# A hybrid decoder block: the last group's gathered rows go to another buffer, a group sooner, and its weights are made ahead of the merges

## The chip, the cores and the metric

The kernel runs on one core of a Trainium2 chip. It is written by hand for the core's engines: PE (TensorE, matrix products into PSUM banks), ACT (ScalarE), DVE (VectorE), POOL (GpSimd, here mostly the issuer of indirect gathers) and SP (SyncE, which issues direct loads and stores; ACT issues some as well). Each engine works through its own instructions in the order written; semaphores order them across engines. The metric is the time of one execution on the device in microseconds, the median over several runs; lower is better.

## The reference

One layer on 256 tokens of width 2048, in float32. First token mixing (RG-LRU and Mamba-2 heads between two projections), then a PEER mixer, then a final norm. The change touches only the end of the PEER mixer and the final norm:

```python
def peer(h, w_q, sub_keys, u_tab, v_tab):
    ...                                  # product keys: 16 experts of 128*128 for each of 8 heads
        u = jnp.take(u_tab, e, axis=0)
        act = jax.nn.gelu(jnp.einsum("td,thkd->thk", xt, u).astype(jnp.float32))
        v = jnp.take(v_tab, e, axis=0)
        return jnp.einsum("thk,thkd->td", (g * act).astype(v.dtype), v)
...
    return x + gate2 * peer(h2, peer_w_q, peer_sub_keys, peer_u, peer_v)
...
    return rms_norm(x, final_norm_g)
```

So each token needs a weighted sum of 8 x 16 = 128 rows of `v_tab` (2048 numbers each), whose weights are the gate times the gelu of a score, the score being the product of the token with a row of `u_tab`.

## The kernel before

**Two ways to one sum.** The kernel orders the experts with the second key's index as the slow one. Experts with slow index below `J1 = 80` are done *sparsely*: all scores of all tokens with these experts are computed as dense products and stored in DRAM (`ad`); then, token by token, the 128 scores and the 128 rows of `v_tab` that the token needs are gathered by indirect DMA. The other 48 slow indices (`JD = 48`) are done *densely*: scores with all of them (`u_slot`), a matrix of weights `Wt[0]`, `Wt[1]` (24 slow indices each, 128 x 24 x 256), and then dense products with the value table (`v_slot`), in two column halves `h` of 48 slots each.

**The sparse part.** Tokens go in 64 groups of four, one for each 32-row strip of the output tile; groups 0 to 31 make the first 128 tokens (`tb` = 0), groups 32 to 63 the second. For a group `q`:

- `w_gather` (line 1370) issues one gather of 128 scores, a column of the tile `wA`; four make a group. `v_gather` (line 1362) issues one gather of 128 rows, 8 KB each, into one of eight buffers `vs[n % 8]`, so two groups lie in memory at a time. Numbers past the table are left out by the bounds check (they are the dense ones). Both go to POOL's queue.
- `w_make` (line 1379) makes the four weight columns: a gelu on ACT (line 1383), then a product with the gates on DVE into `Wz` (line 1387). `Wz` has three places (`NW = 3`), and the columns around the four are zero, so that a window of 32 columns moves each token's sum to its own row of the strip.
- `v_quad` (line 1389) does 16 products on PE (line 1397): for each of four column blocks `c` (one PSUM bank each), the four tokens `g`. Token `g` uses PE's columns and the bank's rows 32 g to 32 g + 31, so neighbouring products go to different strips of PE. Each product is float32 and makes two matmul records. The sums stay in four banks over 32 groups.

`sparse()` (line 1409) does a group: one score gather, `v_quad`, then row and score gathers in turn, for the rows of group q + 2 and the scores ahead. Its weights for the next group are put on the list `late` and made at the next `tick`. A row gather waits until PE has read the buffer that it fills.

**The dense part.** `v_slot` (line 1470) first splits a later slot's weights into a high and a low part (`split_to`, ACT line 442 and DVE line 443), then does 12 matmuls on PE (line 1483) into four banks, two for each half of the tokens, then issues the splitting of a later value tile (`issue_split`, ACT line 144, DVE line 153), whose DVE step also issues the next load.

**The order around the change.** `tick` (line 1421) is called twice in each dense score slot and once after each value slot, 192 times in all; it decides by the count whether a `sparse()` comes, in the second part about once in three value slots. Group 61 comes just before the last value slot; groups 62 and 63 come behind it, at the end of the kernel. `mid()` runs steps that were deferred. `merge(tb, c, ps)` (line 1503) multiplies a bank by the gate (1505), adds it to the rows of the residual `R["t"]` (1507), and when both sums of a column block are in, takes the squares on ACT (1510). It is done for four banks behind the last value slot of each half, and for four banks behind groups 31 and 63. `final(tb)` (line 1512) multiplies two column blocks by the norm's weights (1516), makes the root (1518 to 1520), scales and stores: two blocks by ACT (1525), two by DVE (1523), and three stores on SP (1526, 1527). At the end the order before is: weights of 63, deferred steps, `final(0)`, group 63 with its merges, `final(1)`.

Of the kernel before, what the change touches and what calls it, by code (L numbers as in the profile page):

```python
# [15 lines left out]
OP = mybir.AluOpType  # L16
# [42 lines left out]
def hybrid_kernel(ctx, tc, xT, cols, w_ada, w_in, lru_w, w_o1, w_o2, w_q, keys, u_t, v_t, fng, out):  # L59
# [1299 lines left out]
    def tok(q, g):  # L1359
        return (q // 32) * 128 + 32 * g + q % 32  # L1360

    def v_gather(n):
        q, g = divmod(n, 4)
        if q >= 64:
            return
        x, t = vs[n % 8], tok(q, g)
        pool.indirect_dma_start(x, None, vf, bass.IndirectOffsetOnAxis(ap=eV[:, t:t + 1], axis=0),  # L1367
                                bounds_check=E1 - 1, oob_is_err=False)
# [9 lines left out]

    def w_make(q):
        if q >= 64:  # L1380
            return
        a = wA[:, 4 * q:4 * q + 4]
        act.activation(a, a, AF.Gelu_apprx_tanh)
        tb, m = divmod(q, 32)
        g = gT[:, tb * 128:(tb + 1) * 128].rearrange("p (g m) -> p g m", g=4)[:, :, m]
        o = Wz[:, 32:].rearrange("p (n c) -> p n c", c=32)[:, 4 * (q % NW):4 * (q % NW) + 4, 0]
        dve.tensor_tensor(o, a, g, op=OP.mult)  # L1387

    def v_quad(q):
        tb, m = divmod(q, 32)  # L1390
        if m == 0:
            for c in range(4):
                sb[c] = bank(c)
        for c in range(4):
            for g in range(4):
                x = 32 + 32 * (4 * (q % NW) + g) - m
                pe.matmul(sb[c][32 * g:32 * g + 32, :], Wz[:, x:x + 32], vs[4 * (q % 2) + g][:, c * 512:(c + 1) * 512],  # L1397
                          start=(m == 0), stop=(m == 31), skip_group_check=True)
        if m == 31:
            for c in range(4):  # L1400
                merge(tb, c, sb[c])
# [7 lines left out]
    def sparse():  # L1409
        q = sq["n"]  # L1410
        if q < 64:
# [3 lines left out]
            for g in range(4):  # L1415
                if g:
                    w_gather()
                v_gather(4 * q + 8 + g)
# [51 lines left out]
    def v_slot(h, jj):  # L1470
# [8 lines left out]
        for tb in range(2):  # L1479
            s = slice(tb * 128, (tb + 1) * 128)  # L1480
            for i, k in ((0, 0), (1, 0), (0, 1)):
                for c in range(2):
                    pe.matmul(ob[tb * 2 + c], w[:, i, s], v[:, k, c * 512:(c + 1) * 512],  # L1483
                              start=(jj == 0 and (i, k) == (0, 0)), stop=(jj == JD - 1 and k == 1))
        if jj == JD - 1:
# [17 lines left out]
    def merge(tb, c, ps):  # L1503
# [5 lines left out]
        if R[tb, c] == 2:  # L1509
            act.activation(ps, a, AF.Square, accum_out=rf[:, tb, c:c + 1])  # L1510

    def final(tb):
        a, fn, rows = R["t"][:, tb], R["t"][:, 2], out[tb * 128:(tb + 1) * 128, :]
        for c in range(2):
# [52 lines left out]
    while sq["n"] < 63:  # L1567
        tick()
        sparse()
    tick()  # L1570
    mid()
    mid()
    final(0)
    sparse()
# [70 lines left out]
```

## Time and profile before

| what | value |
|---|---|
| median of 3 runs | 2152.05 us (2142.25 to 2161.91) |
| the profiled execution, its own time | 2157.51 us |
| its span | 2155.8 us |
| PE busy | 2085.5 us, 97% of the span |
| DVE, ACT, POOL busy | 1397.8, 964.9, 887.8 us |
| DMA | 620.54 MB, mean 288 GB/s |
| line 1397 (sparse sums on PE) | 2048 matmul records, two for each product |
| line 1483 (dense sums on PE) | 1152 matmul records, 276.9 us busy |
| score gathers, row gathers on POOL | 256 and 256 |

How to read it: times are microseconds from the start of the span. "PE" is the matmul, "PEld" the loading of its weights, which runs beside it. Behind a row, in brackets, stands how long the engine had been idle before it and what ended that idle time; "issue" means nothing that the profile shows. The ends of matmuls are modelled, and some matmul records can be missing. A row that names POOL with DMA_INDIRECT is the issuing of a gather, not its transfer. Names such as `tk` and `vq` are the eight row buffers (0 to 3 and 4 to 7), `X` in a score gather is the tile `wA`, `H` at the end is the tile of the residual rows.

### The profile page before, as it was taken

Reading aid. Unit: us, or ns where it says so; the run is one execution under the profiler, and the core shown is the slowest. Engines: PE = TensorE matmul, PEld = TensorE weight load, DVE = VectorE, ACT = ScalarE, POOL = GpSimd, SP = SyncE. Lnnn points to the kernel's source line nnn. Section 1 sums busy time; section 2 is a strip of 40 time slices with the busy share of each in tenths; the row PEclk is TensorE's granted clock in tenths of the full one; section 3 lists DMA queues with packets and bytes.
Section 4 is the critical chain, followed back from the end, with each engine's and each line's share of the span. In section 5 each row is a group of like instructions: output and inputs, shape, how many; then the busy total and the mean of one; then the engine's idle time right before and its main releaser. Section 6 shows DMA issues by size and latency. Waiting matters only on the chain.

```text
span 2155.8 us, 34802 instructions
## 1 busy us (share of the span) xinstructions
PE 2085.5 (97%) x13060; PEld 1633.2 (76%) x13060; DVE 1397.8 (65%) x2009; ACT 964.9 (45%) x1472; POOL 887.8 (41%) x728
## 2 busy tenths in 40 slices
PE   7999999999999999999999999999999999999996
PEld 4789989988999898888788778666666656555653
DVE  3378887977888869779889986433334353343434
ACT  3356656666644454444445444333333333333332
POOL 0013133412112110002325641777777757777774
PEclk9999999999999999999999999999999999999998
DMA  9967666767789955677777778899999999999996
GB/s 388 406 224 247 211 218 224 257 223 247 265 306 344 323 181 176 202 242 254 253 259 234 237 266 282 302 360 339 334 348 348 345 329 344 359 371 345 347 342 232
DMA packets 250615, 620.54 MB, mean 288 GB/s; under 512 B 38024, under 2 KB 122168, under 8 KB 228152
## 3 DMA queue, kind: packets, MB, share of 16 engines
q1 hardware_dynamic: 188992, 387.76, 52.0%
q0 software_dynamic: 45056, 175.52, 22.3%
q10 hardware_dynamic: 16400, 55.06, 7.7%
q8 instruction: 102, 1.67, 0.3%
q14 instruction: 65, 0.53, 0.1%
HBM read 696.60 MB, written 14.72 MB: 330 GB/s over the span
## 4 chain that ended last, share of the span: by engine, by line
PE 70%; DMA 9%; DVE 9%; issue 5%; ACT 3%; POOL 2%; another core or an unknown queue 1%; SPq 0%; POOLq 0%; DVEq 0%; ACTq 0%
PE b L449 14%; PE b L1397 9%; PE b L1483 7%; PE b L451 7%; PE b L1323 4%; PE b L1325 4%; PE b L1324 4%; DVE hl L153 4%; PE b L918 3%; DMA raw<-in_w_in 2%; PE b L796 2%; PE b L797 2%; PE b L798 2%; PE b L919 1%; DMA adw<-in_w_ada 1%
## 5 line engine op out<-in xcount | busy, mean ns | idle before, releaser
L144 ACT ACTIVATE hl<-raw 128x1024 fp32r<-128x1024 f32 x594 | 628.0, 1059 | 1058.4 <-PE b L451 198.2
L153 DVE TENSOR_TENSOR hl<-raw,hl 128x1024 fp32r<-128x1024 f32 x594 | 764.7, 1297 | 133.9 <-ACT hl L144 119.5
L449 PE MATMUL b<-H,hl 128*128 128x512 f32 x1376 | 495.1, 403 | 0.1
L451 PE MATMUL b<-H,hl 128*128 128x256 f32 x1376 | 386.8, 281 | 3.9 <-DVE hl L153 3.6
L1376 POOL DMA_INDIRECT X<-ad,X x256 | 297.2, 1161 | 87.7 <-issue 74.4
L449 PEld LDWEIGHTS b<-H,hl 128*128 128x128 f32 x1376 | 259.6, 189 | 87.1 <-issue 19.2
L1483 PE MATMUL b<-hl,X 128*128 128x512 f32 x1152 | 276.9, 397 | 12.3 <-ACT X L442 9.7
L1483 PEld LDWEIGHTS b<-hl,X 128*128 128x128 f32 x1152 | 213.7, 189 | 88.3 <-issue 27.3
L451 PEld LDWEIGHTS b<-H,hl 128*128 128x128 f32 x1376 | 261.0, 190 | 6.5 <-DVE hl L153 5.0
L1323 PE MATMUL b<-hl,H 128*128 128x512 f32 x640 | 253.3, 396 | 0.0
L1325 PE MATMUL b<-hl,H 128*128 128x512 f32 x640 | 250.3, 391 | 2.5 <-DVE hl L153 2.5
L1324 PE MATMUL b<-hl,H 128*128 128x512 f32 x640 | 250.2, 391 | 0.0
L1367 POOL DMA_INDIRECT vq<-in_v_t,X x128 | 150.0, 1172 | 112.8 <-DVE vq L1537 39.0
L1367 POOL DMA_INDIRECT tk<-in_v_t,X x128 | 144.8, 1132 | 70.9 <-issue 32.3
L798 PE MATMUL b<-H,hl 128*128 128x256 f32 x560 | 160.2, 286 | 4.4 <-DVE hl L153 4.4
L796 PE MATMUL b<-H,hl 128*128 128x256 f32 x560 | 163.3, 292 | 0.0
L797 PE MATMUL b<-H,hl 128*128 128x256 f32 x560 | 159.9, 286 | 0.0
L1387 DVE TENSOR_TENSOR Wz<-X 128x4 f32<-128x4 f32 x64 | 10.8, 169 | 224.7 <-DMA X<-ad,X 98.6
L1325 PEld LDWEIGHTS b<-hl,H 128*128 128x128 f32 x640 | 120.6, 188 | 29.2 <-DVE hl L153 4.0
L389 DVE SCALAR_TENSOR_TENSOR adacc<-adr,cact,adacc 128x1024 f32<-128x1024 f32 x90 | 127.6, 1418 | 19.3 <-DMA adr<-in_w_ada 19.0
L1323 PEld LDWEIGHTS b<-hl,H 128*128 128x128 f32 x640 | 120.6, 188 | 23.9
L1324 PEld LDWEIGHTS b<-hl,H 128*128 128x128 f32 x640 | 120.6, 188 | 23.9
(324 smaller groups left out, 3163.2 us busy)
## 6 DMA issues: line engine op xcount, KB each, us to landing
raw<-in_u_t SPq DMA_DIRECT2D x208, 512.0 KB
raw<-in_w_in SPq DMA_DIRECT2D x146, 512.0 KB
adr<-in_w_ada SPq DMA_DIRECT2D x96, 512.0 KB
adw<-in_w_ada SPq DMA_DIRECT2D x64, 512.0 KB
raw<-in_w_o SPq DMA_DIRECT2D x64, 512.0 KB
raw<-in_u_t ACTq DMA_DIRECT2D x48, 512.0 KB
raw<-in_v_t SPq DMA_DIRECT2D x48, 512.0 KB
raw<-in_v_t ACTq DMA_DIRECT2D x48, 512.0 KB
```

Of the source, the lines that this page charges most:

```text
L144: act.activation(t[:, 0], r, AF.Copy)
L153: dve.tensor_sub(t[:, 1], r, t[:, 0].bitcast(FT))
L449: pe.matmul(ps, w[:, 0, c], x[:, k].rearrange("p a b -> p (a b)"), start=(k == first), stop=False, skip_group_check=True)
L451: pe.matmul(ps[:, :256], w[:, 1, c], x[:, k, 0], start=False, stop=(k == 15), skip_group_check=True)
L796: pe.matmul(ps, wh, hT[:, k, 0, :], start=(k == 0), stop=False)
L798: pe.matmul(ps, wl, hT[:, k, 0, :], start=False, stop=(k == 15))
L1323: pe.matmul(o, hh, w[:, 0, :, kk], start=(k == 0), stop=False)
L1324: pe.matmul(o, hl_, w[:, 0, :, kk], start=False, stop=False)
L1325: pe.matmul(o, hh, w[:, 1, :, kk], start=False, stop=(k == 15))
L1367: pool.indirect_dma_start(x, None, vf, bass.IndirectOffsetOnAxis(ap=eV[:, t:t + 1], axis=0), bounds_check=E1 - 1, oob_is_err=False)
L1376: pool.indirect_dma_start(wA[:, n:n + 1], None, adf, bass.IndirectOffsetOnAxis(ap=eW[:, t:t + 1], axis=0), bounds_check=T * E1 - 1, oob_is ...
L1483: pe.matmul(ob[tb * 2 + c], w[:, i, s], v[:, k, c * 512:(c + 1) * 512], start=(jj == 0 and (i, k) == (0, 0)), stop=(jj == JD - 1 and k == 1))
```

## The change

Six edits, all in the sparse part and the end:

- Rows 253, 254 and 255 (tokens 1 to 3 of group 63) go to the place of `Wt[0]`, which holds 3 x 2048 numbers for each partition and is read for the last time about value slot 23 of the second half. Their gathers are issued after group 60, behind its own four; row 252 keeps its buffer and is gathered after group 61.
- At groups 20, 26, 32 and 38 one more score gather is issued, so that from then on scores run four further ahead; the last is issued at group 60.
- In the last value slot, ahead of its merges, the waiting weights (group 62) and those of group 63 are made; `made` keeps them from being made twice.
- `v_quad` takes its 16 products in another order for two groups: group 61 by token (0, 1, 2, 3) with the four column blocks inside, group 63 by token (1, 2, 3, 0).
- The final norm's product for the first two column blocks of the first 128 tokens is done on DVE two deferred steps after their merge, in the middle of the value slots, and no longer in `final(0)`.
- At the end groups 62 and 63 are issued one behind the other, then the deferred steps and `final(0)`, then group 63's four merges and `final(1)`.

```diff
+    def row(n):
+        if n < 253:
+            return vs[n % 8]
+        return Wt[0].rearrange("p a b -> p (a b)")[:, (n - 253) * D:(n - 252) * D]
+
     def v_gather(n):
...
-        x, t = vs[n % 8], tok(q, g)
+        x, t = row(n), tok(q, g)
...
+    made = set()
+
     def w_make(q):
-        if q >= 64:
+        if q >= 64 or q in made:
             return
+        made.add(q)
...
-        for c in range(4):
-            for g in range(4):
-                x = 32 + 32 * (4 * (q % NW) + g) - m
-                pe.matmul(sb[c][32 * g:32 * g + 32, :], Wz[:, x:x + 32], vs[4 * (q % 2) + g][:, c * 512:(c + 1) * 512],
-                          start=(m == 0), stop=(m == 31), skip_group_check=True)
-        if m == 31:
+        order = [(c, g) for c in range(4) for g in range(4)]
+        if q == 61:
+            order = [(c, g) for g in range(4) for c in range(4)]
+        if q == 63:
+            order = [(c, g) for g in (1, 2, 3, 0) for c in range(4)]
+        for c, g in order:
+            x = 32 + 32 * (4 * (q % NW) + g) - m
+            pe.matmul(sb[c][32 * g:32 * g + 32, :], Wz[:, x:x + 32], row(4 * q + g)[:, c * 512:(c + 1) * 512],
+                      start=(m == 0), stop=(m == 31), skip_group_check=True)
+        if q == 31:
             for c in range(4):
                 merge(tb, c, sb[c])
...
-                v_gather(4 * q + 8 + g)
+                if q != 61 or not g:
+                    v_gather(4 * q + 8 + g)
+            if q == 60:
+                for g in range(1, 4):
+                    v_gather(252 + g)
+            if q in (20, 26, 32, 38):
+                w_gather()
             late.append(lambda: w_make(q + 1))
...
+        if (h, jj) == (1, JD - 1):
+            while late:
+                late.pop(0)()
+            w_make(63)
         if jj == JD - 1:
...
         if R[tb, c] == 2:
             act.activation(ps, a, AF.Square, accum_out=rf[:, tb, c:c + 1])
+            if tb == 0 and c < 2:
+                defer(lambda: dve.tensor_tensor(a, a, R["t"][:, 2, s], op=OP.mult), 1)
...
-        for c in range(2):
+        for c in range(2 if tb else 0):
...
-    while sq["n"] < 63:
-        tick()
-        sparse()
-    tick()
-    mid()
-    mid()
+    assert sq["n"] == 62 and {62, 63} <= made
+    sparse()
+    sparse()
+    while any(stages):
+        mid()
     final(0)
-    sparse()
+    for c in range(4):
+        merge(1, c, sb[c])
     final(1)
```

## The prediction

> **What bounds the kernel now.** I read the page, then the second half by stretches, then what TensorE (PE) waited for there, then the last 80 us instruction by instruction.
>
> ```profile
> span 2155.8 us, 34802 instructions
> 2000.00:2100.00 100.00, 99.03 (x570) 61.76 (x573) 40.49 (x59) 35.45 (x58) 74.46 (x66) 1.00 0.97 351
> 2131.00:2156.00 25.00, 9.81 (x64) 2.36 (x64) 14.32 (x27) 8.10 (x18) 4.22 (x5) 0.77 0.50 178
> PE b L1483 <- ACT X L442: 9.7, 5, 3.5
> PE b L1397 <- DVE Wz L1387: 4.0, 1, 4.0
> ```
>
> The stretch rows give length, then busy time of PE, weight loads, DVE, ACT and POOL, the granted clock, the DMA share and GB/s. While the dense and the sparse value sums run together, PE is busy 99.03 of 100 us and DMA 0.97: two limits side by side, with PE ahead. From 2131 on PE works 9.81 of 25 us at a clock of 0.77, and the end is set by waits. The change can win in two places: in the few PE waits of the long stretch, and in this tail.
>
> ```profile
> 2085.69 3.64 PE L1397 MATMUL b<-tk,Wz 128*32 128x512 f32 x32
> 2089.26 8.45 PE L1483 MATMUL b<-hl,X 128*128 128x512 f32 x36
> 2097.64 3.64 PE L1397 MATMUL b<-vq,Wz 128*32 128x512 f32 x32
> 2122.61 4.81 PE L1397 MATMUL b<-vq,Wz 128*32 128x512 f32 x32
> 2127.35 3.06 PE L1483 MATMUL b<-hl,X 128*128 128x512 f32 x12
> 2134.39 5.33 PE L1397 MATMUL b<-tk,Wz 128*32 128x512 f32 x32 [3.98 <-DVE Wz L1387]
> 2139.54 4.78 PE L1397 MATMUL b<-vq,Wz 128*32 128x512 f32 x32
> ```
>
> Columns: start, length, engine, line, names, count, idle before and its releaser. An undisturbed group (v_quad, line 1397) lets the next slot start 3.57 us later (2085.69 to 2089.26), and a dense slot (v_slot) takes (2097.64 - 2089.26) / 3 = 2.79. Counted back from the last one, 2122.61 is group 61, then the last slot, then groups 62 and 63. Group 62 could have followed the slot at about 2130.4 and started at 2134.39; group 63 ended at 2139.54 + 4.78 = 2144.3.
>
> ```profile
> 2134.14 1.00 POOL L1376 DMA_INDIRECT X<-ad,X  x1 [0.30 <-issue]
> 2138.58 0.20 ACT L1383 ACTIVATE X<-X 128x4 f32<-128x4 f32 x1 [6.15 <-DMA X<-ad,X]
> 2122.51 0.99 POOL L1367 DMA_INDIRECT tk<-in_v_t,X  x1 [0.30 <-issue]
> 2127.63 0.99 POOL L1367 DMA_INDIRECT vq<-in_v_t,X  x1 [2.83 <-PE b L1397]
> 2135.44 1.00 POOL L1367 DMA_INDIRECT vq<-in_v_t,X  x1 [0.30 <-issue]
> 2140.70 0.16 PEld L1397 LDWEIGHTS b<-vq,Wz 128*32 128x32 f32 x8 [1.04 <-DMA vq<-in_v_t,X]
> 2128.83 0.70 DVE L1505 TENSOR_TENSOR b<-b,H 128x512 f32<-128x512 f32 x1 [4.48 <-PE b L1483]
> 2133.56 0.69 DVE L1507 TENSOR_TENSOR H<-H,b 128x512 f32<-128x512 f32 x1
> 2138.90 1.29 DVE L1516 TENSOR_TENSOR H<-H 128x512 f32<-128x512 f32 x2
> 2140.82 1.42 DVE L1523 SCALAR_TENSOR_TENSOR H<-H,rf 128x512 f32<-128x512 f32 x2
> 2142.15 0.69 DVE L1505 TENSOR_TENSOR b<-b,H 128x512 f32<-128x512 f32 x1
> 2147.47 1.29 DVE L1516 TENSOR_TENSOR H<-H 128x512 f32<-128x512 f32 x2
> ```
>
> Three things made the tail late. Group 62's weights stood behind the eight merge steps on DVE (2128.83 to 2134.25). Group 63's weights waited for a score gather issued at 2134.14 and used at 2138.58. Group 63's last rows were gathered at 2135.44, after POOL had waited for group 61 (2127.63) and put scores between the rows; PE had them at 2140.70, 5.26 us after issue. After group 63 come four merges on DVE, 2142.15 to 2147.47 = 5.32 us, then 2155.8 - 2147.47 = 8.3 us to the end, which the change leaves alone.
>
> **The change part by part.** *Scores ahead.* Four score gathers move forward, one each at groups 20, 26, 32 and 38; their number stays.
>
> ```profile
> 2098.03 8.70 DMA X<-ad,X
> 1844.00 0.20 ACT L1383 ACTIVATE X<-X 128x4 f32<-128x4 f32 x1 [1.82 <-DMA X<-ad,X]
> 1844.56 1.66 PE L1483 MATMUL b<-hl,X 128*128 128x512 f32 x6 [1.87 <-ACT X L442]
> 1857.09 0.20 ACT L1383 ACTIVATE X<-X 128x4 f32<-128x4 f32 x1 [1.86 <-DMA X<-ad,X]
> 1857.65 1.66 PE L1483 MATMUL b<-hl,X 128*128 128x512 f32 x6 [0.80 <-issue]
> 2106.83 0.20 ACT L1383 ACTIVATE X<-X 128x4 f32<-128x4 f32 x1 [1.50 <-DMA X<-ad,X]
> 2107.39 3.01 PE L1483 MATMUL b<-hl,X 128*128 128x512 f32 x12 [0.44 <-ACT X L442]
> 1985.44 1.89 PE L1483 MATMUL b<-hl,X 128*128 128x512 f32 x7 [2.98 <-ACT X L442]
> POOL tk L1367 <- PE b L1397: 21.4, 10, 7.9
> ```
>
> The first row is from the chain of waits: a score gather took 8.70 us to land, behind rows of values. Then the gelu of line 1383 waits at the head of ACT, the dense split (line 442) behind it comes late, and PE stops: 1.87 + 0.80 + 0.44 = 3.11 us in all. With three scores ahead at the first and four at the other two the gather lies up to a whole group (12 us) earlier, more than 8.70, so these stops go. Late next are the raw dense tiles: the stop of 2.98 at 1985 has no score wait before it. DMA at 0.97 leaves 3 us in each 100 for PE to run ahead. The bounds are 0 (all given back there) and 3.11; I take 2, nearer to 3.11, since over 100 us lie between the early stops and 1985. Each gather costs POOL 1.30 us (1.00 + 0.30 idle) once, delaying the rows behind it; POOL waited 21.4 us for PE in such rows, which hides it. Without that cover it is 1.3 us once for each.
>
> *Last weights ahead of the merges.* Two gelus (0.2 each) and two products on DVE pass eight merges. They run while PE is in the last slot, where DVE waited 4.48 us, so they cost nothing; the 3.98 us before group 62 goes. Group 63's last score is now issued one POOL step (1.30) before 2122.51, and with 8.70 it lands by 2129.9. Queued behind that wait, on ACT and DVE, are the merges; nobody on PE waits for them, so it costs only if the last slot's results are there before about 2130.
>
> *Rows.* Rows 253 to 255 go out behind 2122.51 at steps of 1.30, and row 252 follows at 2122.51 + 4 x 1.30 = 2127.7. With 5.26 to 8.70 it is there at 2133.0 to 2136.4.
>
> *Product of two column blocks ahead.* The first L1516 pair (1.29) leaves the tail and goes to the middle, on a DVE busy 40 us of 100: nothing, or 1.3 once if the split behind it is short. It never set the end.
>
> *Order within groups 61 and 63.* This is the added cost. Before, four neighbouring matmuls go to four different 32-column strips of PE. Now one strip gets its four banks in a row, and then the next.
>
> ```profile
> 2086.14 0.13 PEld L1397 LDWEIGHTS b<-tk,Wz 128*32 128x32 f32 x4 [0.30 <-issue]
> 2086.57 0.13 PEld L1397 LDWEIGHTS b<-tk,Wz 128*32 128x32 f32 x4 [0.30 <-issue]
> 189.52 0.43 PE L577 MATMUL b<-Dm,xdt 128*64 128x128 f32 x2
> 189.79 0.27 PE L578 MATMUL b<-Dm,xdt 128*64 128x128 f32 x1
> 189.79 0.32 PE L577 MATMUL b<-Dm,xdt 128*64 128x128 f32 x1
> 190.01 0.27 PE L579 MATMUL b<-stmp,xdest 128*64 128x128 f32 x1
> ```
>
> Weights come in fours every 0.43 us: a record takes 0.43 on its strip, four strips work at once, and a group's 32 records make 8 rounds, 3.44 us. With one strip's 8 records in a row, everything depends on whether PE starts the next strip while records of the first still wait. The nearest case is y_pe, lines 577 to 579: two records of each line for one half of the columns, then two of each for the other half. The other half's first record (the second 189.79 row) starts with the first half's third of six, ahead of its two L579 records (190.01 and later). So PE does look past waiting matmuls, but not past four: past three. Read so, each next strip starts when the one before is at its fifth of eight, 4 x 0.43 = 1.72 us later, and a group grows by 3 x 1.72 = 5.16 us. The bounds are 0 (looks past all) and 3 x 7 x 0.43 = 9.03 (past none). I take 5.16, the price of the only row of this kind.
>
> **The sum.** Group 61 starts at 2122.61; the slot follows at + 3.57 + 5.16 = 2131.34; group 62 at + 2.79 = 2134.13; group 63 at + 3.44 = 2137.57; its end is + 3.44 + 5.16 = 2146.17, with all weights and rows in place and no pause that lowers the clock. Bank 0 is complete six rounds (2.58) earlier, at 2143.6; DVE needs 5.32: 2148.9 against 2147.47, so + 1.45. Taking off 2 for the scores leaves - 0.55. The profiled execution took 2157.51 us for its span of 2155.8, so 2156.96 on its account; it lies 5.5 above the median of the three runs, 2152.05, and from that median the forecast is **2151.5**. Group 61 lost 4.74 - 3.57 = 1.17 us to a pause with no releaser; I let it go, and + 1.2 if it recurs.
>
> **The rivals.** *Look-ahead without a limit.* Against it: the 0.27 us by which the other half in y_pe starts late. For it: there the matmuls are short. Then the reordered groups cost nothing: slot 2126.18, group 62 at 2128.97, group 63 at 2132.41. Now DVE and row 252 set the end: dense merges finish 2134.25 - 2127.35 = 6.9 after slot start, 2133.1; the first half's scaling takes 2140.82 + 1.42 less the end of L1516 (2140.19) = 2.05: 2135.15; four merges to 2140.5. That is 7.0 under 2147.47, with the scores 9.0: **2143**. Row 252 at its latest (2136.4) needs its strip until 2139.8, and adds 2. The Trainium skill (TensorE: Matmul & The Clock Gate, the table of specifications) gives PE's queue as 64 deep with a partial reorder window. A group is 64 instructions, so by that depth alone this rival would hold; no run here shows that depth.
>
> *Strict order, on the slower side.* A matmul that must wait for its strip holds all behind it. Then each reordered group grows by 9.03: slot 2135.21, group 62 at 2138.0, group 63 at 2141.44, its end 2153.9, bank 0 at 2151.3, merges 2156.65: + 9.2, less 2: + 7.2, **2159**. The kernel is slower than before from 5.4 us a group on: at 5.16 the sum stands at - 0.55, and each us more counts twice. Against it stands 189.79 before 190.01. The Trainium skill (same page, Part 3: Packing small matmuls — row/col tiling) states this rule: matmuls start and end strictly in program order, and only weight loads are pulled ahead. By that rule the end is this rival's; the rows of y_pe disagree.
>
> *The scores' gain is given back.* The stops move to the raw tiles, at DMA 0.97: the 2 us go, + 1.45: **2153.5**. The same time comes if the scores still land too late.
>
> **The numbers.** Forecast 0.50, unlimited look-ahead 0.25, gain given back 0.15, strict order 0.10. All lie within 0.5%. A change of under 1% (21.5 us) can hardly be told from none here, as the three runs reach from 2142.25 to 2161.91. Faster by over 1% needs three times the best rival's gain: 0.03; slower by over 1%, some mishap in the long stretch: 0.03; within 1%: 0.94. The range reaches from rival one to strict order, with about 3 us for the scatter of runs on either side: 2140 to 2162.
>
> **What would show it.** Groups 61 and 63 last about 8.7 us from first to last record with strips starting 1.7 apart (3.5 and 12.5 in the rivals); no wait between the last slot and group 62; PE clock 1.00 until the end of group 63; no stop behind L1383 after 1845. The forecast is wrong if those groups last under 5 or over 11 us, if row 252 is late, or if PE stops more than before between 1850 and 2110.

## The result, and the profile after

| | us |
|---|---|
| kernel before, median of 13 runs | 2154.63 (2142.25 to 2161.91) |
| changed kernel, median of 13 runs | 2165.46 (2156.26 to 2185.14) |
| ratio, 95% interval | 1.0054 (1.0036 to 1.0073) |
| forecast | 2151.5, range 2140 to 2162 |
| profiled execution before / after | 2157.51 / 2167.20 (span 2155.8 / 2165.5) |

The change made the kernel about 11.6 us slower (0.0054 of 2154.63). That is within 1%, as forecast, but the time lies above the range. Line numbers move in the changed kernel: the strips' matmuls are L1409 (L1397 before), the dense matmuls L1501 (L1483), a row gather L1372 (L1367), a score gather L1381 (L1376), the gelu of the weights L1391 (L1383), their product L1395 (L1387), the merges L1527 and L1529 (L1505 and L1507). In the experiments the numbers shift again by a few lines; the names in a row tell the operation (`in_v_t` is a gather of rows, `ad` one of scores, `Wz` the sparse products). ACT's copy that begins a dense split stays L442, and the one that begins the split of a value tile stays L144.

The stretch rows of the changed kernel (length; busy time of PE, weight loads, DVE, ACT, POOL; granted clock; DMA share; GB/s):

```profile
2000.00:2100.00 100.00, 98.62 (x553) 62.62 (x552) 39.55 (x58) 34.48 (x58) 68.01 (x66) 1.00 0.95 348
2131.00:2166.00 35.00, 22.48 (x105) 7.50 (x103) 15.66 (x29) 9.11 (x20) 0.99 (x1) 0.90 0.32 125
```

The waits of its PE and ACT from 1340 on (line, what it waited for: us in total, times, longest):

```profile
PE b L1501 <- issue: 6.4, 5, 3.4
PE b L1501 <- ACT X L442: 4.1, 2, 3.0
ACT hl L144 <- remote: 78.3, 18, 10.2
ACT X L442 <- remote: 17.3, 2, 10.6
```

The wait of PE for the weights of group 62 (3.98 us before) is gone, and PE works 22.48 of the last 35 us instead of 9.81 of 25: the two reordered groups are in there. The rows that matter most are the last two. A wait is marked "remote" when the profile finds no instruction that ended at the time of its release; below it is seen that the work waited for had long been done and its signal came late. The waits of the kernel before have the same rows, which the prediction did not read:

```profile
ACT hl L144 <- remote: 67.4, 20, 7.3
ACT X L442 <- remote: 8.2, 2, 4.3
```

The timelines of PE, ACT, POOL and DVE at the end of the changed kernel (start, length, engine, line, shape, count, idle before and its releaser):

```profile
2112.51 3.64 PE L1409 MATMUL b<-tk,Wz 128*32 128x512 f32 x32
2116.08 5.73 PE L1501 MATMUL b<-hl,X 128*128 128x512 f32 x24
2125.17 4.34 PE L1501 MATMUL b<-hl,X 128*128 128x512 f32 x12 [3.35 <-issue]
2129.44 8.86 PE L1409 MATMUL b<-vq,Wz 128*32 128x512 f32 x32
2138.23 3.02 PE L1501 MATMUL b<-hl,X 128*128 128x512 f32 x12
2141.18 3.64 PE L1409 MATMUL b<-tk,Wz 128*32 128x512 f32 x32
2144.64 5.80 PE L1409 MATMUL b<-Wt,Wz 128*32 128x512 f32 x21
2150.32 0.59 PE L1409 MATMUL b<-vq,Wz 128*32 128x512 f32 x1
2151.14 0.59 PE L1409 MATMUL b<-Wt,Wz 128*32 128x512 f32 x1
2151.17 2.31 PE L1409 MATMUL b<-vq,Wz 128*32 128x512 f32 x5
2124.70 0.42 ACT L442 ACTIVATE X<-Wt 128x256 fp32r<-128x256 f32 x1 [10.62 <-remote]
2131.79 0.42 ACT L442 ACTIVATE X<-Wt 128x256 fp32r<-128x256 f32 x1 [6.67 <-remote]
2133.33 0.99 POOL L1372 DMA_INDIRECT vq<-in_v_t,X  x1 [3.61 <-PE b L1409]
2151.81 0.70 DVE L1527 TENSOR_TENSOR b<-b,H 128x512 f32<-128x512 f32 x1 [4.67 <-PE b L1409]
2157.15 1.29 DVE L1540 TENSOR_TENSOR H<-H 128x512 f32<-128x512 f32 x2
```

Group 60 starts at 2112.51, and 53.0 us later the kernel ends; before it was 2155.8 - 2110.34 = 45.5. Groups 61 and 63 last 8.86 us (2129.44) and 8.84 (2144.64 to 2153.48). Nothing waits ahead of group 62 or for row 252. But ahead of the dense slot at 2125.17 PE stood still for 3.35 us, until its weights' split was done (L442 at 2124.70), and the slot then ran at a lowered clock (granted 0.67 from 2125.17 to 2129.44), 4.34 us instead of 3.02. That split waited for the last matmul of the slot that began at 2116.08, which by the trace ended at 2119.10. Its signal is recorded at 2124.68, 5.6 us later, and the next one at 2131.77, 10 us after its matmul.

The trace keeps the times of the signals, so late ones can be counted. Of the 566 PE instructions between the starts of group 0 and group 60 that signal, 285 before and 304 after had no signal recorded within 0.25 us of their end. Of the 604 ahead of group 0 it was 2 and 1, and one of each lies behind the first score gather (issued at 1342.52 in the trace of before, where group 0 starts at 1349.40). ACT's and DVE's signals turn late from the same moment on.

### The profile page after: what moved, and what is told of

It reads as the page before. It is cut to its first block, busy times and chain, and to the rows that moved or that the text cites. A ratio compares the mean times of both kernels' runs of the same rounds, so it can differ in the third digit from the quotient of the medians.

```text
span 2165.5 us, 34802 instructions
## 1 busy us (share of the span) xinstructions
PE 2096.1 (97%) x13060; PEld 1637.6 (76%) x13060; DVE 1398.1 (65%) x2009; ACT 964.4 (45%) x1472; POOL 868.5 (40%) x728
## 4 chain that ended last, share of the span: by engine, by line
PE 72%; DVE 12%; DMA 7%; issue 5%; ACT 3%; another core or an unknown queue 1%; POOL 0%; SPq 0%; DVEq 0%; ACTq 0%; POOLq 0%
PE b L449 13%; PE b L1501 12%; PE b L1409 11%; PE b L451 6%; DVE hl L153 5%; PE b L1325 4%; PE b L1323 4%; PE b L1324 4%; PE b L918 3%; DMA raw<-in_w_in 2%; PE b L796 2%; PE b L798 2%; PE b L797 2%; DMA two<-in_w_ada 2%; PE b L919 1%
## 5 line engine op out<-in xcount | busy, mean ns | idle before, releaser
L144 ACT ACTIVATE hl<-raw 128x1024 fp32r<-128x1024 f32 x594 | 628.0, 1059 | 1051.4 <-PE b L1501 199.2
L1381 POOL DMA_INDIRECT X<-ad,X x256 | 290.0, 1133 | 91.0 <-issue 79.5
L1501 PE MATMUL b<-hl,X 128*128 128x512 f32 x1152 | 276.8, 397 | 10.5 <-issue 6.4
L1501 PEld LDWEIGHTS b<-hl,X 128*128 128x128 f32 x1152 | 215.5, 190 | 84.3 <-issue 34.4
L1372 POOL DMA_INDIRECT vq<-in_v_t,X x125 | 144.6, 1157 | 123.4 <-DVE vq L1561 42.7
L1372 POOL DMA_INDIRECT tk<-in_v_t,X x128 | 137.7, 1076 | 72.9 <-PE b L1409 29.3
L1395 DVE TENSOR_TENSOR Wz<-X 128x4 f32<-128x4 f32 x64 | 10.7, 168 | 209.4 <-ACT X L1391 62.7
L1325 PEld LDWEIGHTS b<-hl,H 128*128 128x128 f32 x640 | 120.5, 188 | 28.9 <-DVE hl L153 3.7
L1409 PE MATMUL b<-vq,Wz 128*32 128x512 f32 x1000 | 136.1, 596 | 3.6 <-issue 1.8
L1323 PEld LDWEIGHTS b<-hl,H 128*128 128x128 f32 x640 | 120.5, 188 | 24.1
```

The source lines that it names most:

```text
L144: act.activation(t[:, 0], r, AF.Copy)
L1323: pe.matmul(o, hh, w[:, 0, :, kk], start=(k == 0), stop=False)
L1325: pe.matmul(o, hh, w[:, 1, :, kk], start=False, stop=(k == 15))
L1381: pool.indirect_dma_start(wA[:, n:n + 1], None, adf, bass.IndirectOffsetOnAxis(ap=eW[:, t:t + 1], axis=0), bounds_check=T * E1 - 1, oob_is ...
L1409: pe.matmul(sb[c][32 * g:32 * g + 32, :], Wz[:, x:x + 32], row(4 * q + g)[:, c * 512:(c + 1) * 512], start=(m == 0), stop=(m == 31), skip_ ...
```

## The experiments

The measurements stem from six occasions, A for the result above and B to F below. Each has its own runs of the kernel before, and kernels are compared only through these. On B, D and F none of the 566 signals was late, in any of the ten traces; on A, C and E 232 to 304 were, in all nine kernels with score gathers. The median of the kernel before follows: 2134.2, 2134.1 and 2134.8 us on B, D and F; 2154.6, 2144.7 and 2144.1 on A, C and E. This split was not foreseen, so the first expectations do not know of it.

| occasion, signals | kernel | ratio to before (95%) | group 0 to 60 | group 60 to end |
|---|---|---|---|---|
| A, late | change | 1.0054 (1.0036, 1.0073) | 765.5 | 53.0 |
| B, on time | e1 both old orders | 0.9986 (0.9971, 1.0000) | 737.3 | 42.1 |
| | e2 group 61 in old order | 0.9979 (0.9963, 0.9996) | 737.6 | 42.8 |
| | e3 rows 253 to 255 late | 1.0007 (0.9991, 1.0023) | 736.7 | 48.0 |
| | e4 before + scores ahead | 0.9994 (0.9978, 1.0011) | 738.9 | 43.5 |
| C, late | e5 change | 1.0046 (1.0029, 1.0063) | 755.3 | 48.0 |
| | e6 both old orders, row 252 moved | 1.0015 (0.9999, 1.0031) | 753.2 | 41.9 |
| | e7 change, last splits elsewhere | 1.0041 (1.0025, 1.0056) | 762.8 | 48.0 |
| | e8 change without scores | 0.9940 (0.9925, 0.9954) | 734.4 | 48.0 |
| D, on time | e9 change, scores ahead only at the end | 1.0019 (1.0008, 1.0030) | 738.6 | 48.0 |
| | e10 as e6, scores as e9 | 1.0007 (0.9996, 1.0018) | 739.5 | 46.8 |
| | e11 before + scores ahead | 0.9986 (0.9972, 0.9999) | 739.2 | 42.6 |
| | e12 change | 1.0003 (0.9991, 1.0014) | 737.7 | 48.0 |
| E, late | e13 change | 1.0061 (1.0039, 1.0082) | 750.8 | 48.0 |
| | e14 as e9 | 1.0048 (1.0030, 1.0067) | 743.9 | 49.9 |
| | e15 before + scores ahead | 1.0029 (1.0012, 1.0046) | 755.6 | 43.5 |
| | e16 strip 0 last | 1.0022 (1.0008, 1.0037) | 758.2 | 41.4 |
| F, on time | e17 as e16, scores as e9 | 1.0009 (0.9997, 1.0021) | 740.1 | 46.7 |
| | e18 as e16 | 0.9976 (0.9963, 0.9990) | 738.3 | 41.6 |

The last two columns are us of the one profiled execution of each; for the kernel before, on A, they are 760.9 and 45.5, and on no other occasion is there a trace of it. One execution need not stand for the median: that of e13 took 2149.43 us with a median of 2157.95, that of e14 2145.24 with 2154.88.

### Occasion B: the orders, the early rows and the scores by themselves

**e1, both old orders:**

```diff
-        if q == 61:
-            order = [(c, g) for g in range(4) for c in range(4)]
-        if q == 63:
-            order = [(c, g) for g in (1, 2, 3, 0) for c in range(4)]
```

> The changed kernel with groups 61 and 63 back in the old order (bank by bank, the four strips side by side); all else stays. Theory S (late signals: the three early row gathers, queued on POOL behind group 60, keep the gathers running to 2129.7, PE's signals for the last two weight splits on ACT come 5.6 and 10 us late, and PE stops 3.35 us ahead of slot 46 and runs that slot at half the clock): the stop ahead of slot 46 stays, because it lies ahead of group 61; the order alone is worth 5.2 us for group 61 (8.86 against 3.64 us) and 5.2 - 2.6 = 2.6 us for group 63, whose first bank was done 2.6 us before its end, so some 7.8 us less than the changed kernel, about 2157.5 us. Theory O (the order is the whole loss, through more than the two groups' own durations): 11 us less, 2154.5 us, and no stop ahead of slot 46. Theory L (the order costs little, because the rows are late anyway): within 2 us of the changed kernel.

3.0 us less than the kernel before (6.2 less to level). The wait for row 252, which the new orders cover, comes out ahead of group 63, and its first matmul rows run at a lowered clock (granted 0.50 from 2112.25 to 2115.60). First POOL's row, then PE's:

```profile
2103.07 0.99 POOL L1372 DMA_INDIRECT vq<-in_v_t,X  x1 [0.30 <-issue]
2112.25 1.03 PE L1405 MATMUL b<-vq,Wz 128*32 128x512 f32 x1 [3.96 <-DMA vq<-in_v_t,X]
```

Even so the tail is 42.1 us against the 48.0 of e3 on the same occasion, which has both new orders. Theory L falls. The change itself was not run on B, so the sizes that S and O give aren't tested here.

**e2, group 61 alone in the old order** (the first two lines of the diff above):

> The changed kernel with group 61 alone back in the old order. Theory S: 5.2 us less than the changed kernel, about 2160.3 us, group 61 in 3.64 us, and row 252 is asked for at the end of group 61, no later than now, since the first strip of four side by side ends with the others. Theory O: 5 to 8 us less, without the stop ahead of slot 46. Theory L: no gain, and a wait for row 252 in front of the last strip of group 63.

4.5 us less than the kernel before. There is no wait for row 252, against L. The gain that S gives to group 61 is in the tail: 42.8 against 48.0, 5.2 us.

**e3, rows 253 to 255 where the kernel before had them:**

```diff
-        if n < 253:
+        if n < 256:
...
-            order = [(c, g) for g in (1, 2, 3, 0) for c in range(4)]
+            order = [(c, g) for g in range(4) for c in range(4)]
...
-                if q != 61 or not g:
-                    v_gather(4 * q + 8 + g)
-            if q == 60:
-                for g in range(1, 4):
-                    v_gather(252 + g)
+                v_gather(4 * q + 8 + g)
```

> The changed kernel with rows 253 to 255 gathered where the kernel before had them, behind group 61 and into the places of rows 245 to 247, and group 63's strips in the order of their arrival; the two orders, the last weights and the scores ahead stay. Theory S: POOL's gathers pause after 2125, the two weight splits on ACT start 2 to 4 us after their matmul's end as in the kernel before, the stop of 3.35 us and the half clock of slot 46 (1.3 us) go: 4 to 5 us less than the changed kernel, about 2161 us, unless the four rows are late for group 63 (the last asked for at about 2135, so landed by 2143, and needed at 2145). Theory O: no change, 2165.5 us, and the stop ahead of slot 46 stays.

1.5 us more than the kernel before, with the same tail as the change has on every occasion but A. Here no slot stopped, so this run says nothing on S. It does say that with the reordered groups the early rows win nothing: the late ones kept no strip waiting.

**e4, the kernel before with the scores ahead:**

```diff
+            if q in (20, 26, 32, 38):
+                w_gather()
             late.append(lambda: w_make(q + 1))
```

> The kernel before with the four additional score gathers at groups 20, 26, 32 and 38 alone. If scores ahead are worth what the prediction gave them: 2 us less than the kernel before, 2152.6 us, and the stops of PE behind the weights' gelu are gone after 1845. If the place of the changed kernel's other loss lies in them (more gathers among the others, more late signals): 2 to 4 us more than the kernel before.

1.3 us less, its interval from 4.7 less to 2.3 more. That agrees with the 2 us, and hardly with a loss of 2 to 4. PE has no stop behind the weights' gelu after 1845, as expected.

### Occasion C: the change again, the tail mended, the splits set free, and no scores

**e5, the change again:**

> The changed kernel once more, unaltered, so that it stands beside the same runs of the kernel before as the experiments. In the four experiments so far every engine's signal came within 0.25 us of its instruction's end, while in the first two traces 240 to 290 of some 600 of PE's signals after 1350 came later than that. Theory C (the 11 us are the sum of two things: the order's own cost, which is always there, and late signals, which are not always there): with signals on time 3 to 5 us more than the kernel before, no stop ahead of slot 46, groups 61 and 63 at 8.8 us; with late signals again about 11 us more. Rival O: 11 us more in either case.

9.9 us more than the kernel before, and 257 signals late. Yet the slot behind group 60 did not stop this time, nor in any other trace of the change: its tail is 48.0 us in e5, e7, e12 and e13. The 53.0 of the first profile is one execution's, and on C the change lost 9.9 us with no such stop in its trace: the stop at 2125 is not what sets the medians apart.

**e6, old orders, and row 252 in the place of a finished split value tile:**

```diff
+        if n == 252:
+            return last[0]
...
+        if (h, jj) == (1, JD - 3):
+            last.append(wp.tile([128, 2, 1024], FT, name="hl", bufs=NHL).rearrange("p a b -> p (a b)"))
+            v_gather(252)
```

> The changed kernel with both old orders, and with row 252 in the place of the split value tile of slot 44, which has no successor, asked for behind slot 45 instead of behind group 61. If the old order's remaining cost is the wait for row 252 (3.96 us ahead of group 63 with both old orders, and the half clock behind it, about 1.7 us): 5 to 6 us less than both old orders gave, so some 6.5 to 8 us less than the kernel before, and no wait ahead of group 63. If the row's time of landing isn't set by when it is asked for: no gain over both old orders, 2 us less than the kernel before.

3.2 us more than the kernel before, and 6.7 less than the change beside it, which is what the tails say (48.0 - 41.9 = 6.1). Row 252 came no earlier, and the tail is that of both old orders (41.9 against 42.1 in e1): no gain over them, as in the second reading, though not the 2 us less that it gave. From e6's POOL and PE timelines:

```profile
2117.38 0.99 POOL L1376 DMA_INDIRECT hl<-in_v_t,X  x1 [0.30 <-issue]
2126.81 0.59 PE L1409 MATMUL b<-hl,Wz 128*32 128x512 f32 x1 [3.17 <-DMA hl<-in_v_t,X]
```

POOL reached this gather 16.9 us behind the start of group 60 (2100.49), exactly as in e1 (2103.07 - 2086.19). It waited for nothing (0.30): its own queue, at 1.30 us a gather, sets the moment, not the buffer. So the row was not asked for earlier, and whether that would have helped isn't tested. The row was used 9.4 us after.

**e7, the last two splits in places that wait for no slot:**

```diff
             t = xw[0][:, n % 2]
+            if n >= len(vq) - 2:
+                t = wp.tile([128, 4, 256], FR, name="raw", bufs=NRAW)[:, 0:2]
```

> The changed kernel with the split weights of slots 46 and 47 in places of raw value tiles instead of the two alternating places, so that ACT's last two splits no longer wait for a signal of PE from slots 44 and 45. With late signals: the stop of 3.35 us ahead of slot 46 and its half clock go, 4 to 5 us less than the changed kernel in the same call. With signals on time: the same as the changed kernel, within 1 us.

1.0041 against 1.0046, six runs each: no gain that can be measured, though the intervals are too wide to exclude one of 4 us. Theory S, that late signals cost the change 4 to 5 us at the last splits, falls with e5, which lost 9.9 us without that stop.

**e8, no score gathers:**

```diff
-        n = sq["w"]
-        if n >= 256:
-            return
-        sq["w"] += 1
-        t = tok(n // 4, n % 4)
...
+        pass
```

> The changed kernel without the 256 gathers of scores; the scores stay zero, so the rows enter with weight zero (this part of the computation is left out). Theory G (the score gathers, 128 elements of 4 bytes each, are what makes signals late): on a chip where the changed kernel's signals are late, they are on time here, and the stretch from the first group to group 60 is shorter by the stops of PE. If the row gathers make them late, they stay late. On a chip with signals on time: PE stops only for the waits that are left, 0 to 4 us less than the changed kernel.

0.9940: 22.7 us less than the change beside it. Late signals fell from 257 to 80, and no wait is marked remote any more. The stretch takes 734.4 us, where the three kernels beside it took 753.2 to 762.8 and those of occasion B 736.7 to 738.9. So the score gathers bring out most of the late signals of C. The stretch of C is 14 to 26 us longer than that of B with the gathers in both, so most of what e8 saves is the price of late signals and not of the gathers themselves. By which way a gather delays a signal isn't shown.

### Occasion D: the scores ahead, taken away and alone, with signals on time

**e9, the scores ahead only at the end**, and **e10**, the same in e6's kernel:

```diff
-            if q in (20, 26, 32, 38):
+            if q in (57, 58, 59, 60):
                 w_gather()
```

> The changed kernel with the four additional score gathers behind groups 57 to 60 instead of behind 20, 26, 32 and 38, so that the scores run ahead only at the end. Theory H (under late signals the scores ahead cost time in the long stretch: the last four kernels with late signals kept 5 to 7 us over the kernel before that their tails don't explain, and these four gathers are the only edit in that stretch): with late signals 5 us less than the changed kernel in the same call. Rival N (the stretch's excess isn't from this edit): the same as the changed kernel, within 2 us. With signals on time: up to 2 us more than the changed kernel.

> The kernel with both old orders and row 252 in the split tile's place, and with the scores ahead only at the end, as in the run above. Theory H with late signals: 2 to 4 us less than the kernel before (its tail is 41.9 us from group 60 against 45.5 of the kernel before). Rival N with late signals: 3 us more, as with the scores ahead. With signals on time: 3 to 6 us less than the kernel before.

e9 took 3.4 us more than the change beside it (e12), a little over the 2 expected. e10 came to 1.5 us more than the kernel before instead of 3 to 6 less. The trace gives a reason that the edit brought with it: the last score gather now stands last in POOL's queue but one. It delays two things, row 252 and the weights of group 63 (DVE L1399, the product of the weights in this kernel):

```profile
2105.79 0.99 POOL L1376 DMA_INDIRECT hl<-in_v_t,X  x1 [0.30 <-issue]
2113.89 0.59 PE L1409 MATMUL b<-hl,Wz 128*32 128x512 f32 x1 [4.68 <-DMA hl<-in_v_t,X]
2112.75 0.17 DVE L1399 TENSOR_TENSOR Wz<-X 128x4 f32<-128x4 f32 x1 [15.36 <-ACT X L1395]
2125.53 1.29 DVE L1543 TENSOR_TENSOR H<-H 128x512 f32<-128x512 f32 x2
```

POOL reached row 252 18.7 us behind the start of group 60 (2087.10) instead of 16.9, but its matmul began 26.8 us behind that start and in e6 26.3, hardly later. The weights are what counts: the merges stand behind them on DVE, which idled until 2112.75 and then did the eight merge steps of the last slot, the first half's scaling and the eight of group 63 with hardly a pause. The pair that follows them (the last row) starts 38.4 us behind group 60, in e6 33.5 (2134.01 - 2100.49); that is the 4.9 us by which the tail is longer. So this edit does not take the scores ahead away cleanly.

**e11, the kernel before with the scores ahead, again** (the diff of e4):

> The kernel before with the four additional score gathers alone, once more. Theory H with late signals: 5 us more than the kernel before. Rival N: within 2 us of it. With signals on time: within 2 us, as measured (0.9994).

3.0 us less (0.2 to 6.0). No trace of the kernel before itself has its signals on time; this one, with only the scores ahead added, comes nearest. Its tail:

```profile
2098.56 3.64 PE L1397 MATMUL b<-vq,Wz 128*32 128x512 f32 x32
2109.14 5.34 PE L1397 MATMUL b<-tk,Wz 128*32 128x512 f32 x32 [4.00 <-DVE Wz L1387]
2114.29 3.81 PE L1397 MATMUL b<-vq,Wz 128*32 128x512 f32 x32
2115.57 0.70 DVE L1507 TENSOR_TENSOR b<-b,H 128x512 f32<-128x512 f32 x1 [3.16 <-PE b L1397]
```

Group 61 takes 3.64 us, not the 4.81 of the trace on which the prediction was built, group 63 waits for no row, and the first merge follows 1.28 us behind its start, since the old order completes the banks one by one.

**e12, the change a third time:**

> The changed kernel a third time, beside the three above. With late signals 9 to 11 us more than the kernel before; with signals on time 2 to 5 us more, which the last strips' order gives (48.0 us from group 60 to the end against 43.5 with the kernel before's tail on time).

1.0003 (0.9991 to 1.0014): with signals on time the change is worth nothing either way, 0.6 us more, which is below the expected 2 to 5. Rival O of e5, 11 us in either case, falls. ACT's waits, and then the rows of the timeline that answer those of the first profile:

```profile
ACT hl L144 <- PE b L1501: 234.2, 91, 5.6
ACT X L442 <- PE b L1501: 7.4, 2, 5.1
```

```profile
2087.81 8.45 PE L1501 MATMUL b<-hl,X 128*128 128x512 f32 x36
2096.20 8.86 PE L1409 MATMUL b<-vq,Wz 128*32 128x512 f32 x32
2104.99 3.01 PE L1501 MATMUL b<-hl,X 128*128 128x512 f32 x12
2107.93 3.64 PE L1409 MATMUL b<-tk,Wz 128*32 128x512 f32 x32
2090.86 0.42 ACT L442 ACTIVATE X<-Wt 128x256 fp32r<-128x256 f32 x1 [5.06 <-PE b L1501]
2118.57 0.70 DVE L1527 TENSOR_TENSOR b<-b,H 128x512 f32<-128x512 f32 x1 [4.66 <-PE b L1409]
```

No wait is marked remote, the three slots behind group 60 run in one piece, and the reordered group still lasts 8.86 us.

### Occasion E: the same pairs with late signals

**e13, the change a fourth time; e14, the diff of e9; e15, the diff of e4; e16, strip 0 last:**

```diff
-        if q == 61:
-            order = [(c, g) for g in range(4) for c in range(4)]
         if q == 63:
-            order = [(c, g) for g in (1, 2, 3, 0) for c in range(4)]
+            order = [(c, g) for c in range(4) for g in (1, 2, 3)] + [(c, 0) for c in range(4)]
```

> The changed kernel, as the comparison for the three runs beside it. With late signals 9 to 11 us more than the kernel before, with signals on time within 2 us of it.

> The changed kernel with the four additional score gathers behind groups 57 to 60. Theory H (with late signals the scores ahead cost time in the long stretch): with late signals 4 to 7 us less than the changed kernel. Rival N (they don't; the excess is the tail's and chance's): within 2 us of it. With signals on time 3 us more than the changed kernel, as the run beside it measured (1.0019 against 1.0003).

> The kernel before with the four additional score gathers alone. Theory H with late signals: 4 to 7 us more than the kernel before. Rival N with late signals: 1 to 3 us less. With signals on time: 1 to 3 us less (0.9994 and 0.9986 so far).

> The changed kernel with group 61 in the old order, and group 63 in an order between the two: strips 1 to 3 side by side, bank by bank, then strip 0 alone, bank by bank. By the traces the three strips last some 3.6 us and the last strip's banks follow 0.86 us apart, so the first bank is done some 4.5 us behind group 63's start against 7.2 with the change's order, unless row 252 comes later than that: 5 + 2.5 = 7 to 8 us less than the changed kernel by the tail, 6 us less than the kernel before with signals on time (2128), and with late signals 2 to 4 us more than the kernel before, as with the other mended tail (1.0015), or about level with it.

The change took 13.1 us more than the kernel before (8.4 to 17.6), where 9 to 11 was expected. e15 took 6.2 more (2.6 to 9.9): the four score gathers alone cost time on this occasion, where on B and D they gave 1.3 and 3.0. Rival N expected a gain and falls; theory H stands on this one run. e14 gave back 2.8 us where H expected 4 to 7; but its tail is 1.9 us longer than the change's, since its late scores hold the weights of group 63:

```profile
2122.61 5.83 PE L1409 MATMUL b<-Wt,Wz 128*32 128x512 f32 x21 [1.69 <-DVE Wz L1395]
```

That leaves some 4.7 for the stretch. Both intervals are 4 us to either side, so e14 alone decides nothing. It also speaks for a second cost: without the scores ahead it still stands at + 10.3 us (6.4 to 14.4) against the kernel before, and its tail is only 4.4 us longer than in A's trace of before. Some 6 us remain that neither the tail nor the scores ahead explain, unless it is scatter. e16 took 8.4 us less than the change, as expected from its tail, and 4.7 more than the kernel before, a little over the 2 to 4 expected.

### Occasion F: the mended tail with signals on time

**e17** is e16 with the diff of e9, **e18** is e16 again.

> The changed kernel with the mended tail (group 61 in the old order, strips 1 to 3 of group 63 side by side and strip 0 alone behind them) and the four additional score gathers behind groups 57 to 60. Theory H with late signals: level with the kernel before or up to 3 us less. Rival N with late signals: 4 to 5 us more, as with the scores ahead. With signals on time: 2 to 4 us less than the kernel before.

> The changed kernel with the mended tail and the scores ahead as the change has them. With signals on time: 5 to 8 us less than the kernel before (the tail 41.4 us from group 60 to the end against 48.0 with the change, and the change level with the kernel before). With late signals: 4 to 5 us more, as measured (1.0022).

e18 took 5.1 us less than the kernel before (2.1 to 7.9): with signals on time it beats the kernel before, which the change does not (e12; it was not run on F). Its last groups:

```profile
2097.46 3.64 PE L1407 MATMUL b<-vq,Wz 128*32 128x512 f32 x32
2101.03 3.01 PE L1499 MATMUL b<-hl,X 128*128 128x512 f32 x12
2103.98 3.64 PE L1407 MATMUL b<-tk,Wz 128*32 128x512 f32 x32
2109.75 2.33 PE L1407 MATMUL b<-Wt,Wz 128*32 128x512 f32 x13 [0.81 <-DMA Wt<-in_v_t,X]
2113.45 0.70 DVE L1525 TENSOR_TENSOR b<-b,H 128x512 f32<-128x512 f32 x1 [3.50 <-PE b L1407]
```

Its first merge comes 2113.45 - 2103.98 = 9.5 us behind the start of group 62, against 2118.57 - 2107.93 = 10.6 in e12, and group 61 is 5.2 us shorter. e17 took 1.9 us more than the kernel before instead of 2 to 4 less, and its trace names the cause:

```profile
2110.86 3.82 PE L1407 MATMUL b<-Wt,Wz 128*32 128x512 f32 x15 [3.74 <-DVE Wz L1395]
```

The scores of group 63, asked for last, hold its weights, and with them the merges behind these on DVE, as in e10. The scores ahead do more here than what the prediction saw in them: they make possible the weights that are made ahead of the merges.

## Why the prediction was wrong, by its own steps

**The orders of groups 61 and 63: right.** Forecast 8.60 us and strips 1.72 apart; measured 8.86 and 8.84, the last strip 2149.86 - 2144.64 = 5.22 = 3 x 1.74 behind the first, and groups of this order last 8.84 to 8.86 us in every trace. Unlimited look-ahead (3.5 us) and strict order (12.5) both fall. The Trainium skill's rule (TensorE: Matmul & The Clock Gate, Part 3: Packing small matmuls — row/col tiling), that matmuls start and end in program order, agrees with these traces neither in the starts nor in the time. What does keep program order is the signals, below.

**The end of the merges: mis-sized.** "Bank 0 is complete six rounds (2.58) earlier" held for the matmul: 2150.32 + 0.59 = 2150.91 against 2153.48. But the merge began at 2151.81, 7.17 behind the start of group 63 and not 6.03. Bank 0's last matmul signals only behind the strip that stands ahead of it in the program, whose last matmul ended at 2151.14 + 0.60 = 2151.74. That is 0.9 us; the rest is the 0.26 by which the group is longer. Against the trace of before the term is 48.0 - 45.5 = + 2.5 instead of + 1.45. Part of that 45.5 was itself lost to late signals: with signals on time the tail of the kernel before with the scores ahead is 42.6 to 43.5 (e11, e4), and the term is + 4.5 to + 5.4. The prediction saw 1.17 us of this as "a pause with no releaser", and let it go.

**The weights ahead of the merges, the rows, the moved product: right.** No wait ahead of group 62 or 63, row 252 asked for at 2133.33 and in place when its strip came at 2149.86, nothing late for the product. With both old orders, row 252 becomes the late one (e1).

**The scores ahead: the step that failed.** "I take 2" stands beside 1.3 and 3.0 us with signals on time (e4, e11). On E, with late signals, the same edit cost 6.2: the term of the sum that stood at - 2 came out as + 6.2. The sum took the stops behind L1383 for all that stood in the long stretch, and priced them from a trace whose signals were late. With signals on time the mechanism is there, but smaller: between 1590 and 2086 the gelu waits for scores 5.8 to 9.5 us without the scores ahead (e9, e10, e17) and 0 to 2.1 with them (e4, e11, e12, e18); PE's stops behind the split (line 442) between 1740 and 2086 come to 0.8 to 1.2 us without them, not 3.11, and to none with them.

On A itself PE's waits behind L442 did fall, from 9.7 to 4.1 us (1340 to 2112). The clause that stops of PE between 1850 and 2110 would prove the forecast wrong looked for such waits, and those listed there did not grow (7.4 us before, 6.0 after). What grew hides inside the sparse groups, which last longer when PE pauses within one, for a row that comes late (as below) or for nothing that the profile shows (group 61 before). Beyond 3.64 us each, groups 0 to 59 together last 13.7 us longer before and 22.5 after; those between 1850 and 2110, 2.2 and 5.9. In e15 it is 10.2, and with signals on time 0 to 2.4 in any trace. From e15, group 45 with the wait in its middle, and ACT's waits:

```profile
1914.75 1.06 PE L1397 MATMUL b<-vq,Wz 128*32 128x512 f32 x6
1917.89 3.62 PE L1397 MATMUL b<-vq,Wz 128*32 128x512 f32 x26 [2.08 <-DMA vq<-in_v_t,X]
ACT hl L144 <- remote: 33.4, 8, 10.6
```

The rival in which the gain is given back named raw tiles; what gave it back came with late signals, and took more than the gain.

**The sum.** The time lies 14.0 us above the forecast. 2.6 of it is the median the forecast was hung on: 2152.05 from three runs, 2154.63 from thirteen. Of the other 11.4, the scores' term would account for some 8.2 (from - 2 to + 6.2, measured on E), the tail for 1.1 to 3.1 (48.0 against 45.5 in A's trace of before and 43.5 in e15's). Together 9.3 to 11.3; e16 and e6 agree, since each keeps what e15 costs and differs from the change by its tail. But these are parts from other occasions, and the split is not shown for A. Its two traces differ by 7.5 us in the tail (53.0 - 45.5) and by 4.6 in the stretch, and 3.4 of the 4.6 lie ahead of group 20 (250.4 us from group 0 before, 253.8 after), where none of the four gathers had been issued. With signals on time the change stands at + 0.6 us (- 1.9 to + 3.0) against the forecast's - 0.55.

**The range** took its width from the rivals on PE and 3 us of scatter. It had no case for a cost of 6 us in the long stretch, only a chance of 0.03 for a mishap there that costs over 1%, although the trace of before has 75.6 us of ACT's waits as remote (67.4 + 8.2).

**Open.** Why the four score gathers cost time when signals are late, and give time when they are not. The profiles show where to look, not more: in the stretch from group 20 to 40, six of the seven traces with these gathers on A, C and E have 87 to 106 of 194 signals late and the seventh (e16) 72; the two without them (before, e14) have 76 and 58. What makes an occasion one of late signals isn't known either; the chip alone does not decide it, since B and C ran on the chip of the same number. The same kernels were measured on both kinds, and the mended tail without the scores ahead was not measured with late signals.

## What to carry to other kernels

Read what the waits are put down to before pricing them: where work long done is named, or a wait is marked as remote, signals come late, and a price read from such a trace may not hold on another occasion, so measure a small edit on more than one. Stops can also hide inside a group that only lasts longer: compare its length with that of an undisturbed one. Where one strip's row comes late, keep the other strips side by side and put only that strip behind them: a strip put in sequence costs 1.74 us here, and its bank's signal waits for all that stands ahead of it in the program. An edit that asks for something earlier gains only if the queue that asks is free to: POOL was not. And moving a request back in a queue delays all that waits for it in order, as the merges behind the weights in e10 and e17.

## What the runs showed of the hardware that was not expected

- On some occasions the signals of PE, ACT and DVE came late, up to 10 us (2121.82 to 2131.77), from the first score gathers on: in 232 to 304 of 566 PE signals, or in 80 without the score gathers. On others, with the same kernels, in none. The stretch then takes 744 to 766 us instead of 737 to 740.
- Matmuls on different strips overtake each other, but their signals don't: bank 0's matmul ended at 2150.91 and its signal came with the next two at 2151.75 to 2151.83, behind a matmul that ended at 2151.74.
